# Attention's value products one head at a time, with high and low parts side by side, in one decoder layer on one Trainium2 core

## The chip, the core and the metric

The kernel runs on one core of a Trainium2 chip. Its engines work side by side, each through its own queue in order: TensorE (PE: matmuls; PEld: the loads of the stationary operand), VectorE (DVE), ScalarE (ACT), GpSimd (POOL), and SyncE (SP), which issues most DMAs. An engine waits for another only through semaphores. The metric is device time in microseconds for one launch; the lower, the better.

## The reference, cut to what matters

One layer of a decoder in float32: 256 positions, width 1024, 8 heads of 64. With one key block of 256 positions, the block-sparse attention is plain causal attention.

```python
proj = x @ w_in                                  # q | k | v | B | C | h | gate_att | gate_conv
q, k = rope(q), rope(k)
p = softmax(causal(q @ k.T / 8))                 # per head
y_att = (p @ v) @ w_attn_out
y_cnv = (B * causal_dwconv3(C * h)) @ w_conv_out
mix = (sigmoid(g_att) * y_att + sigmoid(g_cnv) * y_cnv) @ w_o
x = layer_norm(alpha * x + mix)
u = causal_dwconv3(x @ w_up)
x = layer_norm(alpha * x + (silu(u_gate) * u_val) @ w_down)
```

## The kernel before, in words

**Precision.** Every product is made of float32 operands that are split in two: a high part (`fp32r`, written by a ScalarE copy) and a low part (the rest, a VectorE subtraction). A product is high x high + high x low + low x high. Two forms are used. `mm3` (L303) makes three matmuls into one place. `cols_wide` and `cols_narrow` (L318, L325) put high and low part of the moving operand side by side, so one matmul of 512 columns gives high x high in columns 0 to 255 and high x low in 256 to 511 of a bank, and one of 256 columns adds low x high to the first half. The two halves of the bank are then added on the way out: ScalarE copies the right half to SBUF (`gate_sum_act`, `conv_sum_act`), VectorE adds the left one (`gate_sum_dve`, `conv_sum_dve`).

**Units and slots.** Weights come as a stream of units of 1024 columns, two to a DMA chunk of 1 MB. Unit by unit `slot(u)` (L468) writes the order by hand: first TensorE's products of unit u, then the work that was hung on this slot for TensorE and ScalarE with `at(u, part, ...)`, then ScalarE's high part of unit u+5 (`split_h`, which also issues a DMA two chunks ahead), then VectorE's low part of unit u+4 (`split_l`), then the work that was hung on the slot for VectorE. Engines run these lists in order, and each goes as far ahead as its semaphores allow. `C0` is the first unit after the projections of q, k and v. Below, "slot n" is unit C0 + n: slots 0 to 11 are the convolution's h, C and B, slots 12 to 27 the sixteen gate units, and from slot 28 on come the output products of attention and convolution, the mix (y). Units go in pairs (`two_units`): a wide half for the first unit; a wide half for the second and then both narrow halves.

**Attention.** Heads go in pairs p = 0 to 3 with j = 0, 1 for the head in the pair. The table at L508 says for each pair in which slots it does `masked` (maximum), `exps`, `normalize`, `probs_T` (transposes into two banks), `probs_h` and `probs_l` (one head per slot, in the two slots after the transposes; high and low part of the transposed probabilities go to `PT`, which all pairs share) and `attend`. `attend(p)` (L439) takes as stationary operand the values of both heads of the pair (128 columns) and as moving operand both heads' probabilities (512 columns for the first 128 keys, 256 for the last 128), so that half of the bank, head 0's values with head 1's probabilities and the reverse, isn't used. `attend_h` and `attend_l` in the slot after it take the used quarters (64 rows each) as high and low part to `aT`, which the mix reads.

**Buffers that the change touches.** `PT` has one copy. The `ps` pool has four banks in rotation (scores, transposed probabilities, results of attend); the `acc` pool has four banks for gate and convolution products, so unit n overwrites the bank of unit n-4. The scratch tag `scr` has six buffers in rotation.

Of the kernel before, what the change touches and what calls it, by code (L numbers as in the profile page):

```python
# [12 lines left out]
AF = mybir.ActivationFunctionType  # L13
ALU = mybir.AluOpType

P = 128
S = 256
# [3 lines left out]
HD = 64  # L21
# [116 lines left out]
def layer_kernel(ctx: ExitStack, tc: tile.TileContext, x, wpack, cpack, ln1_g, ln1_b, ln2_g, ln2_b, out):  # L138
    nc = tc.nc
# [10 lines left out]
    def acc_bank(name):  # L150
        return psum.tile([P, 512], F32, tag="acc", name=name)

    def ps_bank(name):
        return ps_pool.tile([P, 512], F32, tag="ps", name=name)

    def scratch(shape, name, bufs=None, tag="scr"):
        return tmp.tile(shape, F32, tag=tag, name=name, bufs=bufs or 6)
# [57 lines left out]
    def low(l, src, h):  # L215
        nc.vector.tensor_tensor(l, src, h.bitcast(F32), op=ALU.subtract)

    def hl_split(h, l, src, eng=None):
        nc.scalar.activation(h, src, AF.Copy)  # L219
        (eng or nc.vector).tensor_tensor(l, src, h.bitcast(F32), op=ALU.subtract)  # L220
# [47 lines left out]
    def w_mix(tap, j):  # L268
        return consts[:, 148 + tap * 4 + j:149 + tap * 4 + j]
# [33 lines left out]
    def mm3(o, ah, al, bh, bl, start, stop):  # L303

        nc.tensor.matmul(o, ah, bh, start=start, stop=False)  # L305
        nc.tensor.matmul(o, ah, bl, start=False, stop=False)  # L306
        nc.tensor.matmul(o, al, bh, start=False, stop=stop)  # L307
# [34 lines left out]
    qk = big.tile([P, 2, 2, AW], F32, tag="rows", name="qk")  # L342
    qkT = big.tile([P, 2, KT, S], F32R, tag="b16", name="qkT")
    vpt = big.tile([P, 3584], F32R, tag="c16", name="vpt")
    vp = vpt[:, 0:2048].rearrange("p (a t n) -> p a t n", a=2, t=2)
    PT = vpt[:, 2048:3584].rearrange("p (a j n) -> p a j n", a=2, j=2)
    aT = big.tile([P, 4, 2, S], F32R, tag="d8", name="aT")
    yT = big.tile([P, 4, 2, S], F32R, tag="e8", name="yT")
# [30 lines left out]
    SB, SM, PR = {}, {}, {}  # L379
# [58 lines left out]

    def attend(p):  # L439

        b = ps_bank(f"av{p}")
        vs = slice(p * P, (p + 1) * P)
        mm3(b, vp[:, 0, 0, vs], vp[:, 1, 0, vs], PT[:, 0, :, 128:384], PT[:, 1, :, 128:384], True, False)
        late = b.rearrange("p (j q) -> p j q", j=2)[:, :, 128:256]
        mm3(late, vp[:, 0, 1, vs], vp[:, 1, 1, vs], PT[:, 0, :, 0:128], PT[:, 1, :, 0:128], False, True)
        PR[p, "o"] = b

    def attend_h(p):
        for j in range(2):
            hs = slice(j * HD, (j + 1) * HD)  # L450
            nc.scalar.activation(aT[hs, p, 0, :], PR[p, "o"][hs, j * 256:(j + 1) * 256], AF.Copy)

    def attend_l(p):
        for j in range(2):
            hs = slice(j * HD, (j + 1) * HD)
            low(aT[hs, p, 1, :], PR[p, "o"][hs, j * 256:(j + 1) * 256], aT[hs, p, 0, :])

    beside = {}  # L460

    def at(u, part, f, *a):
        beside.setdefault(u, {}).setdefault(part, []).append((f, a))

    done = {"h": 0, "l": 0}
    SPLIT_LAST = U["up0"]
# [26 lines left out]

    def evac_v(banks):
        for t in range(2):
            hl_split(vp[:, 0, t], vp[:, 1, t], banks[t])

    C0 = U[(OFF_H, 0)]
    for t in range(2):
        at(C0 + t, "dve", rope, t)  # L500
    for g2 in (0, 2, 1, 3):
        at(C0 + 2, "pe", qk_transpose, g2)
        at(C0 + 3, "act", qk_h, g2)
        at(C0 + 3, "dve", qk_l, g2)

    at(C0 + 4, "pe", scores, (0, 1))
    at(C0 + 9, "pe", scores, (2, 3))
    for p, (m, e, n, tr, av) in enumerate(((5, 6, 8, 11, 14), (7, 8, 14, 15, 18), (10, 11, 17, 19, 22), (12, 13, 21, 23, 26))):  # L508
        at(C0 + m, "dve", masked, p)
        at(C0 + e, "act", exps, p)  # L510
        at(C0 + n, "dve", normalize, p)
        at(C0 + tr, "pe", probs_T, p)
        for j in range(2):
            at(C0 + tr + 1 + j, "act", probs_h, p, j)
            at(C0 + tr + 1 + j, "dve", probs_l, p, j)
        at(C0 + av, "pe", attend, p)
        at(C0 + av + 1, "act", attend_h, p)
        at(C0 + av + 1, "dve", attend_l, p)


    def x_split(k):
# [18 lines left out]
    banks = [[acc_bank(f"{m}{t}") for t in range(2)] for m in "qk"] + [[ps_bank(f"v{t}") for t in range(2)]]  # L540
# [24 lines left out]
    for k in range(1, KT):  # L565
        for m in range(3):
            if k >= KT - 2 and m < 2:
                split(C0 + 2 * (k - KT + 2) + m)
            qkv_passes(k, m, (0, 1), (0, 1, 2))
            if k == KT - 1:  # L570
                if m < 2:
                    evac_rows(m, banks[m])
                else:
                    evac_v(banks[m])
        qkv_split(k + 2)
        if 2 <= k <= 4:
            rope_tables(k - 2)
# [3 lines left out]
    CB = {}  # L581
# [14 lines left out]
        nc.vector.tensor_tensor(z[:, :, 2:S + 2], CB["s", "c", pr], CB["s", "h", pr], op=ALU.mult)  # L596
        CB["z", pr] = z

    def conv2_act(pr):
        t = CB["t", pr] = scratch([P, 2, S], f"ct{pr}")  # L600
        for e in range(2):
            nc.scalar.activation(t[:, e], CB["z", pr][:, e, 2:S + 2], AF.Copy, scale=w_mix(2, 2 * pr + e))

    def conv2_dve(pr):
        z, t = CB["z", pr], CB["t", pr]
        for e in range(2):
            for tap in (1, 0):
                nc.vector.scalar_tensor_tensor(t[:, e], z[:, e, tap:S + tap], w_mix(tap, 2 * pr + e), t[:, e],
                                               op0=ALU.mult, op1=ALU.add)

    def conv3(pr):
        t = CB["t", pr]
# [5 lines left out]
    def conv4_dve(pr):  # L618
        low(yT[:, 2 * pr:2 * pr + 2, 1, :], CB["t", pr], yT[:, 2 * pr:2 * pr + 2, 0, :])

    for pr, (c1, c2, c3, c4) in enumerate(((6, 9, 11, 13), (14, 16, 18, 20))):
        at(C0 + c1, "dve", conv1, pr)
        at(C0 + c2, "act", conv2_act, pr)
        at(C0 + c2, "dve", conv2_dve, pr)
        at(C0 + c3, "dve", conv3, pr)
        at(C0 + c4, "act", conv4_act, pr)
        at(C0 + c4, "dve", conv4_dve, pr)
        for nm, off in (("h", OFF_H), ("c", OFF_C), ("b", OFF_B)):
            for e in range(2):
                at(U[(off, pr)] + e + 2, "act", conv_sum_act, nm, pr, e)  # L630
                at(U[(off, pr)] + e + 2, "dve", conv_sum_dve, nm, pr, e)
# [13 lines left out]
    def gate(j):  # L645
        nc.scalar.activation(gates[:, j % 8, j // 8, :], GB.pop(("s", j)), AF.Sigmoid, bias=bias_gate(j))

    for j in range(16):
        u = U[("g", 0)] + j
        at(max(u + 3, C0 + 17), "act", gate, j)  # L650
        at(u + 2, "act", gate_sum_act, j)
        at(u + 2, "dve", gate_sum_dve, j)


    def two_units(u, names):
# [121 lines left out]
    banks = [acc_bank(f"o0{nh}") for nh in range(2)]  # L777
# [6 lines left out]
    banks = [acc_bank(f"o1{nh}") for nh in range(2)]  # L784
# [136 lines left out]
    for c in range(1, NP // 2):  # L921
        for e in range(2):
# [3 lines left out]
            d = i - 3  # L926
# [122 lines left out]
```

## Time and profile before

| | |
|---|---|
| three runs | 367.34, 367.78, 368.45 us; median 367.78 |
| the profiled execution | 367.38 us, of which the span from first to last instruction is 365.6 |
| mean granted TensorE clock over the span | 0.994 |
| HBM traffic | 68.24 MB read, 1.05 MB written |

In the prediction's extracts, a line of a group gives line of code, engine, operation, written tile <- read tiles, shape and type, count, then busy us and mean ns of one, then the idle time of the engine ahead of it and what ended most of that. A line of the timeline gives start and duration in us and, in brackets, the idle time ahead of it. A line of the chain of waits gives start, duration, engine, written tile and line. A line of the waits gives who waited for what: total us, times, longest.

### The profile page before, as it was taken

The page shows a single profiled execution, that of the slowest core. Times are in us where ns is not written, and L with a number is a line of the kernel's source. Part 1 is how long each engine was busy: PE and PEld are TensorE (multiplying, and loading weights), DVE is VectorE, ACT ScalarE, POOL GpSimd, SP SyncE. Part 2 cuts the span into 40 slices and gives each one's busy share as a digit, 9 for nine tenths or more (in the row PEclk, how much of TensorE's full clock was granted, in tenths as well). Part 3 has the DMA queues.
Part 4 walks back from the last instruction along what each step waited for, and adds up shares of the span by engine and source line. Part 5 has one row for each costly group of instructions (what it writes and reads, how often), then busy time and mean ns, then how long its engine had stood idle before and what let it go on. Part 6 is the DMA issues. An engine that isn't in the chain of part 4 may idle for free.

```text
span 365.6 us, 5224 instructions
## 1 busy us (share of the span) xinstructions
PE 356.8 (98%) x1964; PEld 309.4 (85%) x1964; DVE 296.8 (81%) x510; ACT 222.7 (61%) x380; POOL 13.5 (4%) x34
## 2 busy tenths in 40 slices
PE   8999999999999999999999999999999999999991
PEld 8888888888898888888888888888888888888891
DVE  4885888779986669989769888977768697999884
ACT  4775777576977666653357676664737475767400
POOL 2000000000000003401100000000000000000000
PEclk9999999999999999999999999999999999999997
DMA  8988465335645634588160845447180917663011
GB/s 270 348 296 329 166 230 192 135 117 199 261 163 183 232 115 127 223 331 287 69 230 20 326 136 210 158 189 277 68 329 24 331 57 295 231 229 117 2 57 57
DMA packets 11240, 69.61 MB, mean 190 GB/s; under 512 B 1232, under 2 KB 1616, under 8 KB 4176
## 3 DMA queue, kind: packets, MB, share of 16 engines
q1 hardware_dynamic: 10496, 67.00, 49.6%
q0 software_dynamic: 576, 2.10, 1.7%
q8 instruction: 15, 0.25, 0.3%
q10 hardware_dynamic: 144, 0.20, 0.1%
q14 instruction: 9, 0.07, 0.1%
HBM read 68.24 MB, written 1.05 MB: 190 GB/s over the span
## 4 chain that ended last, share of the span: by engine, by line
PE 98%; DVE 1%; DVEq 0%; issue 0%
PE pb L323 20%; PE pb L330 10%; PE g L323 8%; PE d L305 5%; PE d L306 5%; PE d L307 5%; PE g L330 4%; PE y L323 4%; PE q L546 3%; PE k L546 3%; PE v L546 3%; PE b L323 2%; PE y L330 2%; PE c L323 2%; PE o L305 2%; PE o L307 2%
## 5 line engine op out<-in xcount | busy, mean ns | idle before, releaser
L197 DVE TENSOR_TENSOR wl<-raw,wh 128x1024 fp32r<-128x1024 f32 x99 | 121.1, 1225 | 26.2 <-ACT wh L192 25.8
L192 ACT ACTIVATE wh<-raw 128x1024 fp32r<-128x1024 f32 x99 | 103.6, 1054 | 28.0 <-DMA raw<-in_wpack 28.0
L323 PE MATMUL pb<-x1T,wh 128*128 128x512 f32 x320 | 76.2, 390 | 0.0
L323 PEld LDWEIGHTS pb<-x1T,wh 128*128 128x128 f32 x320 | 59.7, 188 | 12.1
L330 PEld LDWEIGHTS pb<-x1T,wl 128*128 128x128 f32 x320 | 41.0, 191 | 1.6
L330 PE MATMUL pb<-x1T,wl 128*128 128x256 f32 x320 | 41.5, 283 | 0.0
L220 DVE TENSOR_TENSOR wl<-raw,wh 128x1024 fp32r<-128x1024 f32 (+1 forms) x29 | 27.3, 982 | 7.8 <-ACT wh L219 7.5
L323 PE MATMUL g<-xT,wh 128*128 128x512 f32 x128 | 31.7, 394 | 0.0
L305 PE MATMUL d<-wh,f 128*128 128x512 f32 x80 | 31.3, 391 | 0.0
L306 PE MATMUL d<-wl,f 128*128 128x512 f32 x80 | 31.3, 391 | 0.0
L307 PE MATMUL d<-wh,f 128*128 128x512 f32 x80 | 31.1, 389 | 0.0
L219 ACT ACTIVATE wh<-raw 128x1024 fp32r<-128x1024 f32 (+1 forms) x29 | 23.7, 860 | 10.7 <-DMA raw<-in_wpack 6.6
L323 PEld LDWEIGHTS g<-xT,wh 128*128 128x128 f32 x128 | 23.2, 189 | 4.4
L835 DVE SCALAR_TENSOR_TENSOR fc<-fb,consts,fc 128x254 f32<-128x254 f32 x40 | 19.3, 483 | 1.4
L833 DVE SCALAR_TENSOR_TENSOR fc<-fb,consts,fc 128x255 f32<-128x255 f32 x40 | 19.1, 477 | 0.0
L827 ACT ACTIVATE fc<-fb,consts 128x256 f32<-128x256 f32 x40 | 18.0, 497 | 1.7 <-DVE fb L821 1.7
L817 ACT ACTIVATE fb<-pb 128x512 f32<-128x512 f32 x20 | 11.8, 589 | 9.9 <-PE pb L330 9.8
L307 PEld LDWEIGHTS d<-wh,f 128*128 128x128 f32 x80 | 15.0, 188 | 3.2
L305 PEld LDWEIGHTS d<-wh,f 128*128 128x128 f32 x80 | 15.1, 189 | 2.7
L306 PEld LDWEIGHTS d<-wl,f 128*128 128x128 f32 x80 | 15.1, 189 | 2.6
L330 PEld LDWEIGHTS g<-xT,wl 128*128 128x128 f32 x128 | 16.4, 191 | 0.6
L330 PE MATMUL g<-xT,wl 128*128 128x256 f32 x128 | 16.6, 283 | 0.0
(181 smaller groups left out, 576.8 us busy)
## 6 DMA issues: line engine op xcount, KB each, us to landing
raw<-in_wpack SPq DMA_DIRECT2D x55, 1024.0 KB, 5.0
raw<-in_wpack SPq DMA_DIRECT2D x6, 896.0 KB, 5.9
xr<-in_x SPq DMA_DIRECT2D x1, 1024.0 KB, 7.6
ln<-in_ln_g POOLq DMA_DIRECT2D x2, 512.0 KB, 5.5
ln<-in_ln_b POOLq DMA_DIRECT2D x2, 512.0 KB, 6.1
raw<-in_wpack SPq DMA_DIRECT2D x3, 256.0 KB, 3.2
raw<-in_wpack SPq DMA_DIRECT2D x1, 512.0 KB, 5.8
out<-x SPq DMA_DIRECT2D x2, 256.0 KB, 2.0
```

Source lines behind the costliest of these rows:

```text
L192: nc.scalar.activation(units[u]["h"], raw_of(u), AF.Copy)
L197: nc.vector.tensor_tensor(units[u]["l"], raw_of(u), units[u]["h"].bitcast(F32), op=ALU.subtract)
L219: nc.scalar.activation(h, src, AF.Copy)
L220: (eng or nc.vector).tensor_tensor(l, src, h.bitcast(F32), op=ALU.subtract)
L305: nc.tensor.matmul(o, ah, bh, start=start, stop=False)
L306: nc.tensor.matmul(o, ah, bl, start=False, stop=False)
L307: nc.tensor.matmul(o, al, bh, start=False, stop=stop)
L323: nc.tensor.matmul(bank, un["h"][:, k, n0:n0 + P], b[:, k].rearrange("p a s -> p (a s)"), start=k == 0, stop=False)
L330: nc.tensor.matmul(bank[:, 0:S], un["l"][:, k, n0:n0 + P], b[:, k, 0], start=False, stop=k == nk - 1)
L546: nc.tensor.matmul(banks[m][t], (xl if p == 2 else xh)[:, k, t * P:(t + 1) * P], wl if p == 1 else wh, start=k == 0 and p == 0, stop=k == ...
L833: nc.vector.scalar_tensor_tensor(c[:, 1:S], pb[:, a * S:a * S + S - 1], w_ffn(1, j), c[:, 1:S], op0=ALU.mult, op1=ALU.add)
L835: nc.vector.scalar_tensor_tensor(c[:, 2:S], pb[:, a * S:a * S + S - 2], w_ffn(0, j), c[:, 2:S], op0=ALU.mult, op1=ALU.add)
```

## The change

`attend` works head by head, each into a bank of its own. The values lie in `vp` as four blocks of 64 columns a pair: high of head 0, low of head 0, low of head 1, high of head 1. A head's stationary operand is its two neighbouring blocks; the moving operand is that head's probabilities, high and low part side by side. The bank then has high x high, high x low and low x high in three of its four quarters (the fourth isn't used). For each head, ScalarE copies two of them to SBUF (`attend_out`), one of these copies moving to the other 64 partitions; GpSimd adds the two for both heads; a slot later VectorE adds the third from the bank (`attend_sum`); then `attend_h` and `attend_l` work on 128 rows at once, from SBUF.

In the slots, `at_once` puts each gate's sigmoid and its bank sums ahead of all other work hung on the slot. Pair 3's normalize, transposes and attend go from slots 21, 23, 26 to 19, 21, 24. The second convolution's steps go from slots 14, 16, 18, 20 to 15, 18 and 21 (one half each), 22, 24.

```diff
-    vp = vpt[:, 0:2048].rearrange("p (a t n) -> p a t n", a=2, t=2)
+    vp = vpt[:, 0:2048].rearrange("p (t g n) -> p t g n", t=2, g=4)
...
     def attend(p):
-        b = ps_bank(f"av{p}")
-        vs = slice(p * P, (p + 1) * P)
-        mm3(b, vp[:, 0, 0, vs], vp[:, 1, 0, vs], PT[:, 0, :, 128:384], PT[:, 1, :, 128:384], True, False)
-        late = b.rearrange("p (j q) -> p j q", j=2)[:, :, 128:256]
-        mm3(late, vp[:, 0, 1, vs], vp[:, 1, 1, vs], PT[:, 0, :, 0:128], PT[:, 1, :, 0:128], False, True)
-        PR[p, "o"] = b
+        PR[p, "o"] = [ps_bank(f"av{p}_{j}") for j in range(2)]
+        for j in range(2):
+            b = PR[p, "o"][j]
+            js = slice(j * P, (j + 1) * P)
+            nc.tensor.matmul(b, vp[:, 0, p, js], PT[:, :, j, 128:384], start=True, stop=False)
+            nc.tensor.matmul(b.rearrange("p (a q) -> p a q", a=2)[:, :, 128:256], vp[:, 1, p, js], PT[:, :, j, 0:128],
+                             start=False, stop=True)
+
+    def attend_out(p):
+        c = PR[p, "c"] = scratch([P, 2, S], f"ac{p}")
+        for j in range(2):
+            b, hs, ls = PR[p, "o"][j], slice(j * HD, (j + 1) * HD), slice((1 - j) * HD, (2 - j) * HD)
+            nc.scalar.activation(c[hs, 0], b[hs, S:2 * S], AF.Copy)
+            nc.scalar.activation(c[hs, 1], b[ls, 0:S], AF.Copy)
+        nc.gpsimd.tensor_tensor(c[:, 0], c[:, 0], c[:, 1], op=ALU.add)
+
+    def attend_sum(p):
+        c = PR[p, "c"]
+        for j in range(2):
+            hs = slice(j * HD, (j + 1) * HD)
+            nc.vector.tensor_tensor(c[hs, 0], PR[p, "o"][j][hs, 0:S], c[hs, 0], op=ALU.add)

     def attend_h(p):
-        for j in range(2):
-            hs = slice(j * HD, (j + 1) * HD)
-            nc.scalar.activation(aT[hs, p, 0, :], PR[p, "o"][hs, j * 256:(j + 1) * 256], AF.Copy)
+        nc.scalar.activation(aT[:, p, 0, :], PR[p, "c"][:, 0], AF.Copy)

     def attend_l(p):
-        for j in range(2):
-            hs = slice(j * HD, (j + 1) * HD)
-            low(aT[hs, p, 1, :], PR[p, "o"][hs, j * 256:(j + 1) * 256], aT[hs, p, 0, :])
+        low(aT[:, p, 1, :], PR[p, "c"][:, 0], aT[:, p, 0, :])
...
+    def at_once(u, part, f, *a):
+        beside.setdefault(u, {}).setdefault(part, []).insert(0, (f, a))
...
     def evac_v(banks):
         for t in range(2):
-            hl_split(vp[:, 0, t], vp[:, 1, t], banks[t])
+            b = banks[t].rearrange("p (g j d) -> p g j d", g=4, j=2)
+            o = vp[:, t].rearrange("p g (a d) -> p g a d", d=HD)
+            hl_split(o[:, :, 0:4:3], o[:, :, 1:3], b)
...
-    for p, (m, e, n, tr, av) in enumerate(((5, 6, 8, 11, 14), (7, 8, 14, 15, 18), (10, 11, 17, 19, 22), (12, 13, 21, 23, 26))):
+    for p, (m, e, n, tr, av) in enumerate(((5, 6, 8, 11, 14), (7, 8, 14, 15, 18), (10, 11, 17, 19, 22), (12, 13, 19, 21, 24))):
...
         at(C0 + av, "pe", attend, p)
-        at(C0 + av + 1, "act", attend_h, p)
-        at(C0 + av + 1, "dve", attend_l, p)
+        at(C0 + av + 1, "act", attend_out, p)
+        at(C0 + av + 2, "dve", attend_sum, p)
+        at(C0 + av + (4 if p == 0 else 3), "act", attend_h, p)
+        at(C0 + av + (4 if p < 2 else 3), "dve", attend_l, p)
...
-    for pr, (c1, c2, c3, c4) in enumerate(((6, 9, 11, 13), (14, 16, 18, 20))):
+    for pr, (c1, c2, c3, c4) in enumerate(((6, (9, 9), 11, 13), (15, (18, 21), 22, 24))):
...
-    for j in range(16):
+    for j in reversed(range(16)):
         u = U[("g", 0)] + j
-        at(max(u + 3, C0 + 17), "act", gate, j)
-        at(u + 2, "act", gate_sum_act, j)
-        at(u + 2, "dve", gate_sum_dve, j)
+        at_once(u + 2, "act", gate_sum_act, j)
+        at_once(u + 2, "dve", gate_sum_dve, j)
+        at_once(max(u + 3, C0 + 17), "act", gate, j)
```

More of the change, by code (lines that the diff above doesn't have):

```diff
@@ L439, in attend, with attend_h @@
     def attend(p):
-        b = ps_bank(f"av{p}")
-        vs = slice(p * P, (p + 1) * P)
-        mm3(b, vp[:, 0, 0, vs], vp[:, 1, 0, vs], PT[:, 0, :, 128:384], PT[:, 1, :, 128:384], True, False)
-        late = b.rearrange("p (j q) -> p j q", j=2)[:, :, 128:256]
-        mm3(late, vp[:, 0, 1, vs], vp[:, 1, 1, vs], PT[:, 0, :, 0:128], PT[:, 1, :, 0:128], False, True)
-        PR[p, "o"] = b
-    def attend_h(p):
+        PR[p, "o"] = [ps_bank(f"av{p}_{j}") for j in range(2)]
[14 more added lines that the diff above has]
+        c = PR[p, "c"]
         for j in range(2):
             hs = slice(j * HD, (j + 1) * HD)
-            nc.scalar.activation(aT[hs, p, 0, :], PR[p, "o"][hs, j * 256:(j + 1) * 256], AF.Copy)
+            nc.vector.tensor_tensor(c[hs, 0], PR[p, "o"][j][hs, 0:S], c[hs, 0], op=ALU.add)
+    def attend_h(p):
+        nc.scalar.activation(aT[:, p, 0, :], PR[p, "c"][:, 0], AF.Copy)
     def attend_l(p):
-        for j in range(2):
-            hs = slice(j * HD, (j + 1) * HD)
-            low(aT[hs, p, 1, :], PR[p, "o"][hs, j * 256:(j + 1) * 256], aT[hs, p, 0, :])
+        low(aT[:, p, 1, :], PR[p, "c"][:, 0], aT[:, p, 0, :])
     beside = {}
@@ L597, in conv1, with conv2_act, conv2_dve @@
         CB["z", pr] = z
[L599 to L604, printed above, removed]
+    def conv2_act(pr, e):
+        if e == 0:
+            CB["t", pr] = scratch([P, 2, S], f"ct{pr}")
+        nc.scalar.activation(CB["t", pr][:, e], CB["z", pr][:, e, 2:S + 2], AF.Copy, scale=w_mix(2, 2 * pr + e))
+    def conv2_dve(pr, e):
         z, t = CB["z", pr], CB["t", pr]
[L606 to L609, printed above, removed]
+        for tap in (1, 0):
+            nc.vector.scalar_tensor_tensor(t[:, e], z[:, e, tap:S + tap], w_mix(tap, 2 * pr + e), t[:, e],
+                                           op0=ALU.mult, op1=ALU.add)
     def conv3(pr):
@@ L619, in conv4_dve @@
         low(yT[:, 2 * pr:2 * pr + 2, 1, :], CB["t", pr], yT[:, 2 * pr:2 * pr + 2, 0, :])
-    for pr, (c1, c2, c3, c4) in enumerate(((6, 9, 11, 13), (14, 16, 18, 20))):
+    for pr, (c1, c2, c3, c4) in enumerate(((6, (9, 9), 11, 13), (15, (18, 21), 22, 24))):
         at(C0 + c1, "dve", conv1, pr)
-        at(C0 + c2, "act", conv2_act, pr)
-        at(C0 + c2, "dve", conv2_dve, pr)
+        for e in range(2):
+            at(C0 + c2[e], "act", conv2_act, pr, e)
+            at(C0 + c2[e], "dve", conv2_dve, pr, e)
         at(C0 + c3, "dve", conv3, pr)
```

## The prediction

> **What bounds the kernel now.** I read the page first: busy time, then the chain that ended last.
>
> ```profile
> span 365.6 us, 5224 instructions
> ...
> PE 356.8 (98%) x1964; PEld 309.4 (85%) x1964; DVE 296.8 (81%) x510; ACT 222.7 (61%) x380; POOL 13.5 (4%) x34
> ...
> PE 98%; DVE 1%; DVEq 0%; issue 0%
> ```
>
> TensorE is busy for 98% of the span and is 98% of the chain. Busy matmul time alone proves little, since ends are modelled, so I asked next for TensorE's waits and then for the stage that the change touches (from the first gate products to the mix).
>
> ```profile
> PE warm L234 <- DVE zeros L224: 1.0, 1, 1.0
> ```
>
> ```profile
> 76.00:128.50 52.50, 52.50 (x314) 46.71 (x314) 41.63 (x82) 38.47 (x77) 0.00 (x0) 1.00 0.53 197
> ```
>
> The first is the whole list of TensorE's waits: one, at the start. In the second (PE, PEld, DVE, ACT, POOL busy, granted clock, DMA share, GB/s) TensorE has no gap in 52.5 us, at a granted clock of 1.00, while VectorE idles 52.5 - 41.63 = 10.9 us and ScalarE 14.0 us. So a matmul that goes shortens the kernel by its own spacing, and nothing else in the change can shorten it; work added to the others costs nothing until TensorE meets it late.
>
> **What goes.** The chain of waits around the third pair's attend (p=2) gives the spacings; there are four, by the count of the group below.
>
> ```profile
> 109.01 1.84 PE g L323 x8
> 110.85 0.23 PE av L305
> 111.08 0.23 PE av L306
> 111.30 0.23 PE av L307
> 111.53 0.12 PE av L305
> 111.64 0.12 PE av L306
> 111.76 0.12 PE av L307
> 111.88 1.84 PE g L323 x8
> 113.72 1.91 PE g L330 x16
> 115.64 0.11 PE ptp L428
> ```
>
> ```profile
> L305 PE MATMUL av<-vpt 128*128 128x512 f32 x4 | 1.6, 389 | 0.0
> ```
>
> Three products of 512 columns at 0.23 us and three of 256 at 0.12 fill 111.88 - 110.85 = 1.03 us. Afterwards there are two of each (one of either kind a head): a third of 1.03, 0.34, goes, and 4 x 0.343 = 1.38 us in all. The transposes and every other product stay, in number and size; those of p=3 only move two units forward.
>
> The alternation is new: 512, 256, 512, 256 instead of three and three, each with its own weight load.
>
> ```profile
> L330 PEld LDWEIGHTS g<-xT,wl 128*128 128x128 f32 x128 | 16.4, 191 | 0.6
> ```
>
> A load takes 0.19, yet sixteen narrow products follow each other at 1.91 / 16 = 0.12, so loads overlap; I take the spacings as they are. If each 256-column product had to stand for its full load, a head would cost 0.23 + 0.19 and the four attends would save only 4 x (1.03 - 0.84) = 0.8 us. That is the low end of this term; no row lets a product be quicker, so 1.4 is the other.
>
> By the Trainium skill (TensorE: Matmul & The Clock Gate, "Wait — 56ns, not 53.3ns?") a warm product of N columns follows after N / 2.4 GHz and about 2.5 ns, 216 ns for 512. By that page's figure my estimate of the saving would be 4 x (0.216 + 0.109) = 1.30 us instead of 1.38; the trace's 0.23 is wider, and the trace decides.
>
> **What is added, and what covers it.** Per pair: ScalarE had two 64-row copies and gets four and one of 128 rows; VectorE had two 64-row subtractions and gets two 64-row sums and one 128-row subtraction; GpSimd gets one sum.
>
> ```profile
> L451 ACT ACTIVATE aT<-av 64x256 fp32r<-64x256 f32 x8 | 3.0, 378 | 5.6 <-PE av L307 5.5
> L696 ACT ACTIVATE mT<-m 128x256 fp32r<-128x256 f32 x8 | 3.3, 418 | 5.2 <-POOL m L693 5.2
> L216 DVE TENSOR_TENSOR mT<-m,mT 128x256 fp32r<-128x256 f32 x8 | 3.3, 417 | 0.0
> L693 POOL TENSOR_TENSOR m<-m 128x256 f32<-128x256 f32 x8 | 6.5, 807 | 144.7 <-DVE m L692 144.7
> L817 ACT ACTIVATE fb<-pb 128x512 f32<-128x512 f32 x20 | 11.8, 589 | 9.9 <-PE pb L330 9.8
> ```
>
> ScalarE: 4 x (2 x 0.38 + 0.42) = 4.7 us of 14.0 idle. VectorE: 4 x 0.42 = 1.7 of 10.9. Two of the four copies move 64 rows to the other half of the partitions, which no row shows: below, 0.38 like the straight ones (taken, same engine, bank and size); above, 0.59, the widest bank copy.
>
> GpSimd's sums now fall among VectorE's splits. Once in the present trace the two meet:
>
> ```profile
> 154.18 0.78 POOL L693 TENSOR_TENSOR m<-m 128x256 f32<-128x256 f32 x1 [0.80 <-DVE m L692]
> ```
>
> ```profile
> 154.28 1.76 DVE L197 TENSOR_TENSOR wl<-raw,wh 128x1024 fp32r<-128x1024 f32 x1
> ...
> 156.39 1.22 DVE L197 TENSOR_TENSOR wl<-raw,wh 128x1024 fp32r<-128x1024 f32 x1
> ```
>
> The split beside the sum took 1.76 instead of 1.22, 0.54 more. Four meetings cost VectorE 4 x 0.54 = 2.2 us, at most 4 x 0.81 = 3.2; or the sum waits up to 1.22 for a split. This speaks against the change. With 1.7 it makes 3.9 us of 10.9 idle.
>
> The Trainium skill (SBUF — State Buffer, "SBUF: two separate sides") says that VectorE with two SBUF inputs and GpSimd share a port pair under an exclusive lock, the loser waiting for the whole instruction. The trace agrees in direction: by a full wait for the sum's end at 154.96 the split would have taken 0.68 + 1.22 = 1.90, and took 1.76. By that rule the four meetings would be 4 x 0.68 = 2.7 us in place of 2.2, an estimate inside the bound above.
>
> **Who is late next.** Slots are units counted from C0. Splits run far ahead, banks less, probabilities least:
>
> ```profile
> 108.56 0.42 DVE L643 TENSOR_TENSOR gs<-g,gs 128x256 f32<-128x256 f32 x1
> ...
> 110.78 1.23 DVE L197 TENSOR_TENSOR wl<-raw,wh 128x1024 fp32r<-128x1024 f32 x1 [0.33 <-ACT wh L192]
> ...
> 119.28 0.55 DVE L216 TENSOR_TENSOR vpt<-ptp,vpt 128x384 fp32r<-128x384 f32 x1
> ```
>
> ```profile
> 111.72 2.00 PE L323 MATMUL g<-xT,wh 128*128 128x512 f32 x8
> ...
> 123.56 0.39 PE L305 MATMUL av<-vpt 128*128 128x512 f32 x1
> ...
> 126.44 2.08 PE L330 MATMUL g<-xT,wl 128*128 128x256 f32 x16
> ```
>
> The split at 110.78 (slot 23, the last gate unit) is read from 126.44: 14 us of lead. The bank sum at 108.56 (slot 21) ends 2.7 us before 111.72, when unit 23 overwrites that bank; the new order puts this sum ahead of a subtraction and a normalize, so this lead grows. The last probabilities end at 119.83, 3.7 us before attend(3). This lead shrinks, since attend(3) moves from slot 26 to 24 and its transposes from 23 to 21.
>
> Count from the start of attend(2) in slot 22. TensorE reaches attend(3) after the attend, a wide half, the narrow half, a wide half: 0.69 + 1.84 + 1.91 + 1.84 = 6.28 us. ScalarE's first write of p=3's probabilities now overwrites those that attend(2) is reading, a wait that in the old order was two slots away. Behind it in its queue stand that slot's split, then slot 23: gate, bank sum, four copies, the second write; for it VectorE's last subtraction waits, and for that attend(3). Starts of the next instruction give the costs:
>
> ```profile
> 111.92 0.77 ACT L451 ACTIVATE aT<-av 64x256 fp32r<-64x256 f32 x2 [1.18 <-PE av L307]
> ...
> 117.05 1.06 ACT L192 ACTIVATE wh<-raw 128x1024 fp32r<-128x1024 f32 x1
> 118.00 0.49 ACT L434 ACTIVATE vpt<-ptp 128x384 fp32r<-128x384 f32 x1
> 118.37 0.52 ACT L646 ACTIVATE gates<-gs,consts 128x256 f32<-128x256 f32 x1
> 118.77 0.39 ACT L639 ACTIVATE gs<-g 128x256 f32<-128x256 f32 x1
> 119.03 1.08 ACT L192 ACTIVATE wh<-raw 128x1024 fp32r<-128x1024 f32 x1
> ```
>
> Head 0 is read by 0.51 (0.23 and a 256-column product of 0.28); then 0.37 + 0.95 + 0.40 + 0.26 + 2 x 0.77 + 0.49 for ScalarE and 0.55 for VectorE: 5.07. So 1.2 us of lead are left, 0.9 if the wait is for head 1 too, and about 0.5 with copies of 0.59 (2 x 0.21 more; crossing ones only). I take no stall. Without this cover each further microsecond on ScalarE costs one.
>
> ```profile
> 128.51 0.93 PE y L323 x4
> ```
>
> The mix starts at 128.51. After attend(3), which is two units earlier, TensorE does 1.84 + 1.91 + 1.84 + 1.84 + 1.91 = 9.3 us before it; the last pair's copies, sum, sum, high and low parts take 1.54 + 0.81 + 1.22 (a split in the way) + 0.86 + 0.42 + 0.42 = 5.3. Covered. The second convolution's steps move 1 to 5 slots later and end in slot 24, also before the mix; the sums' new place in each slot issues nothing more. No DMA is added, and the issues on SP's queue keep their order behind the splits. The value split after the projections writes 64-column pieces:
>
> ```profile
> L220 DVE TENSOR_TENSOR x1T<-x1t,x1T 128x512 fp32r<-128x512 f32 x4 | 2.7, 686 | 1.2 <-ACT x1T L219 1.1
> ...
> L220 DVE TENSOR_TENSOR vpt<-v,vpt 128x512 fp32r<-128x512 f32 x2 | 1.3, 686 | 0.2 <-ACT vpt L219 0.2
> ```
>
> The first already writes four separate pieces of 128 and takes the 686 ns of the second, which is whole today: nothing.
>
> **The sum.** 365.6 - 1.38 = 364.2 us of span. The profiled execution took 367.38, 1.8 around its span, so 366.0 on its own scale; it lies 0.4 below the shown median of 367.78. On the median's scale the forecast is 367.78 - 1.38 = 366.4.
>
> **Rivals.**
> - *Part of it comes back at attend(3).* For: its lead falls from 3.7 to about 1 us, behind a wait for attend(2). Against: the count above. A slip of 1.5 to 2 us on ScalarE leaves a stall of 0.5 to 1: 366.9 to 367.4.
> - *Weight loads show.* Only 0.8 us goes: 367.0. For: the 0.19 of a load is over the 0.12 of a narrow product. Against: sixteen of those in a row do not show it. In this case the change mostly doesn't do what it says.
> - *Slower: VectorE falls behind in slots 14 to 27.* If its 10.9 us of idle are all waits that stay, the 3.9 us added there push it back by 3.9, and from the point where the lag passes the shortest lead (1.2 us, attend(3)) TensorE pays: 3.9 - 1.2 = 2.7, less 1.38: 369.1. With no lead left, 370.3. For: the meeting of split and sum. Against: the splits that it does there have 14 us of lead, so its waits can shrink.
>
> **How the numbers follow.** The forecast has 0.69, the attend(3) stall 0.13, weight loads 0.06, slower 0.12. Within 0.3% is 366.68 to 368.88, about what this measurement tells from no change. The forecast is only 0.28 us beyond, with a spread of the shown runs of 1.1 us, so I give nine tenths of it to faster: 0.69 x 0.9 = 0.62, with a little from the attend(3) case 0.65. Same: 0.07 + 0.10 + 0.06 = 0.23. Slower 0.12. The range runs from 365.8 (the forecast less the runs' half spread) to 367.8 (a stall that gives all back).
>
> **What would show it.** Per attend, the chain should have 0.23, 0.12, 0.23, 0.12 and 0.69 us in place of 1.03; TensorE's waits should still be the one at the start; the mix's first product should start at 127.1 instead of 128.5; VectorE splits of about 1.76 should stand beside GpSimd's sums. Wrong is the forecast if a wait of TensorE on VectorE appears before attend(3) in slot 24 or before a gate product, or if narrow products next to wide ones start 0.19 apart.

## The result, and the profile after

The changed kernel takes 366.09 us (median of 10 executions, 365.45 to 366.99), the kernel before 367.44 in as many beside it: a ratio of 0.9964, 95% interval 0.9954 to 0.9973. That is 1.35 us, where 1.38 was forecast.

The profiled execution of the changed kernel took 366.63 us. Its page, span and busy time:

```profile
span 364.6 us, 5227 instructions
...
PE 355.4 (97%) x1956; PEld 306.8 (84%) x1956; DVE 297.5 (82%) x514; ACT 226.3 (62%) x392; POOL 16.6 (5%) x38
```

TensorE has 8 products fewer, ScalarE 12 instructions more, VectorE and GpSimd 4 more each. The span fell by only 1.0 us between these two executions, which needs its own look. The list of TensorE's waits, after:

```profile
PE warm L234 <- DVE zeros L224: 1.0, 1, 1.0
PE v L568 <- ACT wh L219: 0.3, 1, 0.3
```

The second wait is new, and it lies in the projections, long before anything that the change touches: a weight's high part came a little later in this execution. The control further below, the same kernel, doesn't have it. The chain of waits of both kernels says where the time went. For each, first the convolution's first product, then VectorE's last sum from a bank; before:

```profile
38.27 3.63 PE h L323 x16
...
357.84 0.43 DVE x L990
```

and after:

```profile
38.61 3.63 PE h L323 x16
...
356.82 0.43 DVE x L1012
```

From one to the other the kernel before takes 357.84 - 38.27 = 319.57 us and the changed one 318.21: 1.36 less. The changed execution only started that stretch 0.34 later. In all the profiles of this study the start lies between 37.47 and 38.73, so this stretch is a far finer measure than the span, and the table of experiments gives it for each.

The chain around the third and fourth attend, after:

```profile
111.21 0.23 PE av L447
111.44 0.12 PE av L448
111.56 0.23 PE av L447
111.79 0.11 PE av L448
111.90 1.82 PE g L323 x8
113.72 1.91 PE g L330 x16
115.64 1.84 PE g L323 x8
117.48 0.23 PE av L447
...
127.51 0.93 PE y L323 x4
```

An attend now fills 111.90 - 111.21 = 0.69 us where it filled 1.03. Wide and narrow products alternate at the same 0.23 and 0.12 as before. The next attend follows 6.27 us later, with no gap. The mix starts at 127.51; less the 0.34 by which this execution was late, that is 127.17, where 127.1 was forecast. The view of the stage by engine, of the same length less what was saved:

```profile
76.00:127.10 51.10, 51.10 (x306) 45.37 (x305) 42.24 (x86) 41.84 (x89) 3.21 (x4) 1.00 0.50 184
```

TensorE is busy throughout again; VectorE went from 41.63 to 42.24 us and ScalarE from 38.47 to 41.84 in a stretch that is 1.4 shorter. What was added has vanished in their idle time.

The last probabilities, whose lead was to shrink most, are seen in the timeline of ScalarE, of VectorE and of TensorE, after:

```profile
111.66 0.49 ACT L435 ACTIVATE vpt<-ptp 128x384 fp32r<-128x384 f32 x1 [3.44 <-PE av L448]
...
115.21 0.49 ACT L435 ACTIVATE vpt<-ptp 128x384 fp32r<-128x384 f32 x1
```

```profile
115.74 0.56 DVE L216 TENSOR_TENSOR vpt<-ptp,vpt 128x384 fp32r<-128x384 f32 x1 [0.94 <-ACT vpt L435]
```

```profile
111.05 0.40 PE L447 MATMUL av<-vpt 128*128 128x512 f32 x1
...
117.32 0.39 PE L447 MATMUL av<-vpt 128*128 128x512 f32 x1
...
117.66 0.40 PE L447 MATMUL av<-vpt 128*128 128x512 f32 x1
```

ScalarE stood still for 3.44 us until attend(2) had been read, the wait that was forecast. The probabilities were complete at 116.30; attend(3) began at 117.32, and its second head, the only one that needs these, at 117.66. (The chain above dates the same products 0.16 us later than the timeline does; starts are compared within one view only.)

### The profile page after: what moved, and what is told of

Its sections match the earlier page's. It is cut to its first block, busy times and chain, and to the rows that moved or that the text cites. A ratio compares the mean times of both kernels' runs of the same rounds, so it can differ in the third digit from the quotient of the medians.

```text
span 364.6 us, 5227 instructions
## 1 busy us (share of the span) xinstructions
PE 355.4 (97%) x1956; PEld 306.8 (84%) x1956; DVE 297.5 (82%) x514; ACT 226.3 (62%) x392; POOL 16.6 (5%) x38
## 4 chain that ended last, share of the span: by engine, by line
PE 96%; DMA 1%; DVE 1%; SPq 0%; ACT 0%; DVEq 0%; issue 0%
PE pb L323 20%; PE pb L330 10%; PE g L323 8%; PE d L305 5%; PE d L306 5%; PE d L307 5%; PE g L330 4%; PE y L323 4%; PE v L568 3%; PE q L568 3%; PE k L568 3%; PE b L323 2%; PE y L330 2%; PE c L323 2%; PE o L305 2%; PE o L307 2%
```

## The experiments

All are compared with the kernel before, run beside them on the same chip. "Stretch" is the one above, from the convolution's first product to VectorE's last sum from a bank, in one profiled execution.

| run | median us (before) | ratio, 95% | stretch us | against before |
|---|---|---|---|---|
| kernel before | | | 319.57 | |
| changed kernel | 366.09 (367.44) | 0.9964 (0.9954 to 0.9973) | 318.21 | -1.36 |
| order alone | 367.40 (367.63) | 0.9988 (0.9976 to 1.0001) | 319.55 | -0.02 |
| four products | 366.14 (367.63) | 0.9960 (0.9943 to 0.9977) | 318.18 | -1.39 |
| sums not ahead | 366.33 (367.63) | 0.9964 (0.9950 to 0.9977) | 318.22 | -1.35 |
| products alone | 366.27 (367.63) | 0.9959 (0.9945 to 0.9973) | 318.24 | -1.33 |
| four copies more | 366.69 (367.51) | 0.9980 (0.9971 to 0.9989) | 318.64 | -0.93 |
| eight copies more | 368.64 (367.51) | 1.0037 (1.0024 to 1.0049) | 320.29 | +0.72 |
| twelve GpSimd sums more | 366.78 (367.51) | 0.9984 (0.9975 to 0.9993) | 318.23 | -1.34 |
| the same again | 366.48 (367.49) | 0.9972 (0.9959 to 0.9986) | 318.21 | -1.36 |
| twelve GpSimd memsets more | 366.48 (367.49) | 0.9976 (0.9966 to 0.9986) | 318.22 | -1.35 |
| changed kernel again | 366.13 (367.49) | 0.9965 (0.9952 to 0.9978) | 318.22 | -1.35 |

### Where the gain is from: order alone, and four products

The first has the new order without the new products, as against the kernel before:

```diff
+    def at_once(u, part, f, *a):
+        beside.setdefault(u, {}).setdefault(part, []).insert(0, (f, a))
...
-... (12, 13, 21, 23, 26))):
+... (12, 13, 19, 21, 24))):
...
-    for pr, (c1, c2, c3, c4) in enumerate(((6, 9, 11, 13), (14, 16, 18, 20))):
+    for pr, (c1, c2, c3, c4) in enumerate(((6, (9, 9), 11, 13), (15, (18, 21), 22, 24))):
...
-    for j in range(16):
+    for j in reversed(range(16)):
-        at(max(u + 3, C0 + 17), "act", gate, j)
-        at(u + 2, "act", gate_sum_act, j)
-        at(u + 2, "dve", gate_sum_dve, j)
+        at_once(u + 2, "act", gate_sum_act, j)
+        at_once(u + 2, "dve", gate_sum_dve, j)
+        at_once(max(u + 3, C0 + 17), "act", gate, j)
```

> The kernel before with the new order only: sums ahead in their slots, pair 3 and the second convolution moved, attend as before with its six products. If the gain is the spacing of the removed products: no change, ratio 1.000 (within 0.0015), each attend still 1.03 us on TensorE, no wait of TensorE. If the order itself brings a part: below 0.9985. If moving attend(3) two slots forward needs the later steps of the change: a wait of TensorE before attend(3) and a ratio above 1.0015.

The second keeps order and layout of the kernel before and only has fewer products:

```diff
-        mm3(b, vp[:, 0, 0, vs], vp[:, 1, 0, vs], PT[:, 0, :, 128:384], PT[:, 1, :, 128:384], True, False)
+        nc.tensor.matmul(b, vp[:, 0, 0, vs], PT[:, 0, :, 128:384], start=True, stop=False)
+        nc.tensor.matmul(b, vp[:, 0, 0, vs], PT[:, 1, :, 128:384], start=False, stop=False)
...
-        mm3(late, vp[:, 0, 1, vs], vp[:, 1, 1, vs], PT[:, 0, :, 0:128], PT[:, 1, :, 0:128], False, True)
+        nc.tensor.matmul(late, vp[:, 0, 1, vs], PT[:, 0, :, 0:128], start=False, stop=False)
+        nc.tensor.matmul(late, vp[:, 0, 1, vs], PT[:, 1, :, 0:128], start=False, stop=True)
```

> The kernel before with the low x high products of each attend left out (four products of six), so its values lack that small term; nothing is added and the order is the old one. If the gain is the spacing of two products for each pair: ratio 0.9962 (1.38 us of 367.44), the same as the change. If weight loads show or the gain lies in the layout or the order: between 0.998 and 1.000.

The order alone moved the stretch by 0.02 us, and its interval takes in 1. The two products by themselves moved it by 1.39, as the whole change does, in an order where six became four of the same kinds in a row rather than in turn. So the gain is the spacing of the products that went, and neither the layout nor the order has a share in it. The chain of this second kernel at its third attend:

```profile
110.06 0.23 PE av L443
110.29 0.23 PE av L444
110.52 0.12 PE av L446
110.63 0.12 PE av L447
```

Four products in 0.69 us, like the alternating ones: weight loads show in neither.

### What of the order is needed: sums not ahead, and products alone

The first takes the gates' sums out of the lead again (the loop of the kernel before, with `at`); the second also puts the second convolution back into slots 14, 16, 18, 20.

> The changed kernel, but gates' sigmoids and bank sums hung behind the other work of their slots, as before. If banks have lead enough (2.7 us in the old order, less the additions ahead of the sums, some 0.8 us): as the changed kernel, 0.9964, no wait of TensorE. If the lead of the sums is needed: waits of TensorE before gate products in slots 22 to 25, and 0.997 to 1.002.

> As the run before, and with the second convolution's steps back in slots 14, 16, 18, 20: only the values' layout, the additions and pair 3's row of the table are new. If the added work has cover everywhere: again 0.9964. If the re-spreading is needed: waits of TensorE before attend(1) or a gate product, since ScalarE has two more copies (0.8 us) in slot 16 ahead of pair 1's probabilities; 0.997 to 1.002.

Both keep the whole gain, and the only wait of TensorE in either is the one at the start. With the added work in place, banks come free in time without the lead, and ScalarE's two copies in slot 16 don't reach the probabilities of pair 1. Only pair 3's new row of the table stays. By the listing it has to: with `attend_out`, `attend_sum` and the two parts in three successive slots, attend(3) in slot 26 would have its result ready in slot 29 only, and the mix reads it from slot 28 on. This wasn't run.

### How far the cover goes: four and eight copies more

`attend_out` of pair 2 (slot 23) repeats its crossing copies, each of the two twice more (four times in the second kernel), as against the changed kernel:

```diff
             nc.scalar.activation(c[hs, 1], b[ls, 0:S], AF.Copy)
+            for i in range(2 if p == 2 else 0):
+                nc.scalar.activation(c[hs, 1], b[ls, 0:S], AF.Copy)
```

> The changed kernel with four more 64x256 copies on ScalarE in slot 23 (attend_out of pair 2 repeats its crossing copies), ahead of pair 3's second write: 4 x 0.39 = 1.57 us. If attend(3) has 1.0 us of lead (the trace of the changed kernel: probabilities end at 116.30, attend(3) starts at 117.32) and each microsecond beyond costs one: a wait of TensorE of about 0.5 us before attend(3), ratio about 0.998. If the cover is wider than it looks: 0.9964 and no wait.

> The same with eight more copies: 3.1 us. With 1.0 us of lead: a wait of about 2.1 us before attend(3), ratio about 1.002, so the gain is gone and more. If a wait is made good later, or the price is less than one for one: below 0.9995.

TensorE's waits, with four copies more and with eight:

```profile
PE av L447 <- DVE vpt L216: 0.2, 1, 0.2
```

```profile
PE av L447 <- DVE vpt L216: 1.8, 1, 1.8
```

In the timelines of the second, TensorE around attend(3), the subtraction that it waits for, and ScalarE's added copies:

```profile
117.22 0.28 PE L448 MATMUL av<-vpt 128*128 128x256 f32 x1
119.32 0.50 PE L447 MATMUL av<-vpt 128*128 128x512 f32 x1 [1.82 <-DVE vpt L216]
119.65 0.28 PE L448 MATMUL av<-vpt 128*128 128x256 f32 x1
```

```profile
118.70 0.56 DVE L216 TENSOR_TENSOR vpt<-ptp,vpt 128x384 fp32r<-128x384 f32 x1 [4.22 <-ACT vpt L435]
```

```profile
114.12 1.62 ACT L459 ACTIVATE ac<-av 64x256 f32<-64x256 f32 x4
...
116.56 1.60 ACT L459 ACTIVATE ac<-av 64x256 f32<-64x256 f32 x4
```

The wait stands before the second head's first product, as the probabilities of the first were ready a slot earlier. The eight copies took 1.62 + 1.60 = 3.22 us and cost 320.29 - 318.21 = 2.08 in the stretch, 1.14 less. The four (0.80 + 0.79) cost 0.43, 1.16 less. From four to eight the stretch grows by 1.65 for some 1.6 us of copies. So behind the lead the price is one for one; a stall here isn't made good later, since TensorE has no idle time to catch up in.

The 1.15 us aren't quite the lead itself, as the starts show. From ScalarE's first write of these probabilities to the end of VectorE's last subtraction the changed kernel takes 116.30 - 111.66 = 4.64 us; with four copies more it is 6.30 (111.22 to 117.52) and with eight 7.93 (111.33 to 119.26), 1.66 and 3.29 longer. The second head's first product follows the narrow one before it after 0.12 us (117.54 to 117.66) in the changed kernel, after 0.46 (117.11 to 117.57) with four copies more and after 2.10 with eight, 0.34 and 1.98 later. So 1.3 us were covered both times. On top of the delay the product that was waited for holds up the next one for some 0.33 us instead of 0.23: having to wait at all costs another 0.1, and the rest is that the copies take a little more of the queue than their busy time.

In the medians the eight copies missed their expectation: the ratio was to be about 1.002, which is what the stretch gives (0.72 us), and came out at 1.0037. That rests on five executions, of which the profiled one was the fastest (368.32 against 368.63 to 368.96 us); where the others lost more isn't known.

### GpSimd beside VectorE: twelve sums, twelve memsets

```diff
         nc.gpsimd.tensor_tensor(c[:, 0], c[:, 0], c[:, 1], op=ALU.add)
+        for i in range(3):
+            nc.gpsimd.tensor_tensor(c[:, 1], c[:, 1], c[:, 1], op=ALU.add)
```

In the kernel with memsets the added line is `nc.gpsimd.memset(c[:, 1, 0:8], 0.0)`.

> The changed kernel with each of GpSimd's four sums followed by three more sums of the same size, whose results nothing reads. If a sum holds a port against VectorE's operations with two inputs in SBUF: several VectorE splits in slots 15 to 27 take 1.5 to 2.0 us instead of 1.22, VectorE's busy time of the stage grows by 2 to 6 us, and since splits have 14 us of lead the time stays at 0.9964 to 0.998. If the engines don't disturb each other here: splits stay at 1.22.

The expectation on VectorE missed. In the stage its busy time was 43.36 us, 1.1 more than in the changed kernel, where 2 to 6 were expected:

```profile
76.00:127.10 51.10, 51.10 (x307) 45.37 (x305) 43.36 (x86) 42.32 (x89) 15.91 (x16) 1.00 0.50 184
```

The repeat of this run, below, gives 43.38, so the 1.1 is no scatter. In this kernel's timeline, the first of GpSimd's added sums beside pair 0, then the three beside pair 1 one by one, and VectorE meanwhile:

```profile
88.06 0.94 POOL L460 TENSOR_TENSOR ac<-ac 128x256 f32<-128x256 f32 x1
...
101.16 0.67 POOL L460 TENSOR_TENSOR ac<-ac 128x256 f32<-128x256 f32 x1
101.91 0.61 POOL L460 TENSOR_TENSOR ac<-ac 128x256 f32<-128x256 f32 x1
102.60 1.68 POOL L460 TENSOR_TENSOR ac<-ac 128x256 f32<-128x256 f32 x1
```

```profile
88.45 1.63 DVE L197 TENSOR_TENSOR wl<-raw,wh 128x1024 fp32r<-128x1024 f32 x1
...
100.83 1.84 DVE L423 TENSOR_SCALAR sm<-sm,st 128x128 f32<-128x128 f32 x4
102.59 1.21 DVE L197 TENSOR_TENSOR wl<-raw,wh 128x1024 fp32r<-128x1024 f32 x1
```

Here whichever of the two engines begins second waits. The split at 88.45 began while the sum of 88.06 ran; it took 1.63 us in place of 1.22 and ended at 90.08, 1.08 after that sum's end at 89.00. At 102.59 it is the other way round. The split began between two sums, just ahead of the third, and took its usual 1.21; the third sum took 1.68 in place of the 0.61 of one that isn't held up, and ended at 104.28, 0.47 after the split's end at 103.80. In both cases the instruction that came second lasts on, after the other's end, for all but 0.14 us of its own time (1.22 - 1.08, 0.61 - 0.47). The other added sums that are caught by a split are alike: they begin at 89.08, 116.53, 122.09 and 124.53, take 1.48 to 1.68 us and end 0.47 us after the split. Begun within 0.01 us of each other, either engine can come first: the last step of the normalize, at 101.90, waited for the sum of 101.91.

As the added sums mostly came second, GpSimd paid most of the price: the twelve took 15.91 - 3.21 = 12.70 us, against 12 x 0.61 = 7.3 unhindered. VectorE's 1.1 is the split's 0.41 and 0.8 in the four steps of pair 1's normalize, 1.84 in place of 1.01, two of which waited for a sum.

In the stretch TensorE didn't wait (its one new wait, of 0.2 us, lies in the projections ahead of it), and the stretch is that of the changed kernel; yet the ratio is 0.0020 worse than the changed kernel's, some 0.7 us, and 0.9984 is beyond the 0.998 that was expected at most. Some 0.5 us of it lies between the issue of the last output transfer and the end of the span. Three more runs bear on this.

> The changed kernel as it is, beside the two runs with additions on GpSimd: 0.9964, and about 3.2 us from the issue of the last output transfer's end to the end of the span, as in its first profile.

> The run with twelve more sums on GpSimd again, on the chip of the control. If the 0.0020 that it lost is real: 0.998 again, with no wait of TensorE and the lost half microsecond behind the last output transfer. If it was the start of those executions: 0.9964, as the control.

> The changed kernel with twelve small memsets (8 columns) on GpSimd in place of the twelve sums. If the half microsecond at the end comes with the number of GpSimd's instructions: 0.998 and the longer end here too. If it comes with their length: 0.9964.

The last issue and the span, in the control and with the memsets:

```profile
span 363.4 us, 5227 instructions
...
359.90 0.37 ACTq L1025 DMA_DIRECT2D out<-x  x1
```

```profile
span 364.7 us, 5236 instructions
...
360.75 0.37 ACTq L1027 DMA_DIRECT2D out<-x  x1
```

From the end of that issue to the end of the span the control takes 363.4 - 360.27 = 3.13 us, the memsets 364.7 - 361.12 = 3.58, and the two executions with sums 3.65 and 3.67. In the eight other profiled executions, none with more on GpSimd than the changed kernel, it is 3.12 to 3.30. So the longer end comes with GpSimd's additional instructions and not with their length. The traces' single instructions, which the views leave out, show where it arises. At the end of the program GpSimd runs a drain behind a semaphore instruction. In the three executions with twelve instructions more, the drain begins 0.42 to 0.44 us after the start of that instruction and takes 0.23; in the nine others it begins 0.08 to 0.09 after it and takes 0.09 to 0.10. That is nearly the whole difference. In the medians it is smaller, 366.48 (sums and memsets alike) against 366.13, with intervals that overlap. What holds GpSimd up there isn't shown and stays open.

## Why the prediction was right

**What bounds.** TensorE was taken to be without a gap, so that each product is worth its own spacing. Right: two products of six, taken out alone, give the same 1.39 us of stretch as the change, and everything else in it gives nothing.

**The saving per attend.** 0.343 us forecast, 1.03 - 0.69 = 0.34 measured; 1.38 in sum against 1.36 in the stretch and 1.35 in the medians. The spacing that alternating products would have was the one unknown of this term, and it is the old spacing. The rival that weight loads show is out.

**The added work.** The straight copies (L456) and the crossing ones (L457), as groups after:

```profile
L457 ACT ACTIVATE ac<-av 64x256 f32<-64x256 f32 x8 | 3.0, 379 | 0.1
L456 ACT ACTIVATE ac<-av 64x256 f32<-64x256 f32 x8 | 3.0, 375 | 0.6 <-PE av L448 0.6
```

Both take the 0.38 that was assumed; the crossing costs nothing, which no row of before could say. The last lead was counted as 5.07 us of queue against 6.28 of TensorE, 1.2 left. The trace gives 116.30 - 111.05 = 5.25 of queue against 6.27, so the queue is 0.18 longer than counted; but the deadline is the second head's product, 0.34 after attend(3) begins. By the doses of copies 1.3 us of lead are there. That the count came so close is in part luck, as the two errors go against each other.

**The bank sums.** It was said that their new place issues nothing more and only lengthens leads. Right, and the leads didn't need it: the kernel without it is as fast.

**The port that VectorE and GpSimd share.** This term was mis-sized. It was put at 0.54 us for each of four meetings, 2.2 in all, on the strength of one split of 1.76 beside a sum. In the changed kernel one VectorE operation shows it clearly, at pair 0, the timelines of GpSimd and VectorE:

```profile
87.48 0.75 POOL L458 TENSOR_TENSOR ac<-ac 128x256 f32<-128x256 f32 x1 [84.89 <-ACT ac L457]
```

```profile
87.89 0.89 DVE L618 TENSOR_TENSOR z<-cc,ch 128x512 f32<-128x512 f32 x1
```

The group of this product in the kernel before:

```profile
L596 DVE TENSOR_TENSOR z<-cc,ch 128x512 f32<-128x512 f32 x2 | 1.4, 684 | 0.0
```

So 0.2 us went: the product ended 0.55 after the sum's end at 88.23, again all but 0.14 of its own time. The other three sums fell beside operations that read a bank or beside shorter ones, and once the sum came second: it began at 121.28, during a subtraction of 0.42 us, and itself took 0.98. So the mechanism was right, and also that either a split or a sum may be the one that waits. The size failed because no split happened to begin during a sum, as all four were priced. The Trainium skill's rule (SBUF — State Buffer, "SBUF: two separate sides") that the loser waits for the whole instruction fits every meeting looked at here, but for the first 0.14 us of the one that waits. It fits the split of 1.76 too, which the prediction took to agree in direction only: 154.28 + 1.76 = 156.04 is 1.08 after the sum's end at 154.96, as for the split at 88.45. As the cover of VectorE was 10.9 us wide, the size of the term had no bearing on the time.

**The rivals.** The stall at attend(3) didn't come, but it was the nearest: some 1.3 us further on ScalarE and it begins. The slower case needed a lag of VectorE that passes the leads in front of it; its waits for ScalarE's high parts shrank instead, as was argued. The lists of waits in the stage, before and after:

```profile
DVE wl L197 <- ACT wh L192: 4.3, 10, 0.5
```

```profile
DVE wl L197 <- ACT wh L192: 2.0, 5, 0.7
```

## What to carry to other kernels

Where one engine runs without a gap, work moved from it to engines with idle time is worth exactly the spacing of the instructions that go, read from the chain of waits rather than from their durations (here 0.23 and 0.12 us, against durations of 0.39 and 0.28). Whether the moved work has cover is then a question of the shortest lead in front of the bound engine, which can be counted in advance by adding the starts along one queue from a common event. To test such a count, lengthen the queue by a known dose, twice: the two losses give the price and, but for what having to wait at all costs, the lead (here 1.15 us by the losses, 1.3 by the starts).

## What the runs showed of the hardware that wasn't expected

A ScalarE copy of 64 partitions x 256 from a bank isn't followed as closely as one of 128 partitions: the next instruction starts 0.38 to 0.40 us later at a duration of 0.37 to 0.38, whereas the bank sums' 128-row copies of the same length are followed after 0.26. In the changed kernel's timeline of ScalarE:

```profile
113.39 0.38 ACT L661 ACTIVATE gs<-g 128x256 f32<-128x256 f32 x1
113.65 0.37 ACT L456 ACTIVATE ac<-av 64x256 f32<-64x256 f32 x1
114.03 0.38 ACT L457 ACTIVATE ac<-av 64x256 f32<-64x256 f32 x1
114.42 0.38 ACT L456 ACTIVATE ac<-av 64x256 f32<-64x256 f32 x1
114.81 0.38 ACT L457 ACTIVATE ac<-av 64x256 f32<-64x256 f32 x1
```

It goes by the copy and not by what follows. The 128-row copy at 113.39 is followed after 0.26 although the next one has 64 rows and reads a bank as well; the last 64-row copy is followed after 0.40 although the next, the write of the probabilities at 115.21, has 128 rows. Two half-height copies cost 0.78 us of queue, one of full height 0.26.

A VectorE operation and a GpSimd sum that both work from SBUF held each other up for the whole of the one that began first, less 0.14 us, in whichever order they came (splits of 1.63 in place of 1.22, sums of 1.68 in place of 0.61).

The end of the program grew by some 0.5 us in the profiles when GpSimd got twelve more instructions in the middle of it, whether these were sums or memsets of 8 columns; the time goes to GpSimd's last drain.
